# Spacers that move the start addresses of the 256-column matmul operands in retention and attention

## The chip, the cores and the metric

The kernel runs on one core of one Trainium2 chip. The metric is the device time of one execution in microseconds; lower is better. Three timed runs of the kernel before gave a median of 1052.99 us (1051.14 to 1053.38). One more execution was profiled; it took 1049.72 us, of which 1047.6 us lie between its first and its last instruction.

## What is computed

The reference is one encoder layer over 1040 positions (16 learned meta tokens ahead of 1024 inputs) of width 1024, in float32:

```python
u = rms_norm(h);  z = u @ w_in            # one projection of 7680 columns, cut in ten parts
o_r = retention(q, k, v)                  # 4 heads, dk 128, dv 256; chunks of 128; both directions, own decays
y_r = (group_norm(o_r) * silu(rg)) @ w_rb
o_a = attention(q, k, v)                  # 8 heads, 2 key groups, window +-128, 16 meta keys, a sink logit
y_a = (o_a * silu(ag)) @ w_ab
out = (sigmoid(gr) * y_r + sigmoid(ga) * y_a) @ w_o
h + rms_norm(out)                         # meta tokens dropped
```

## The kernel before, in words

Every product of float32 matrices is made of three matmuls, because each operand is split into a high part and a low part: `mm3` (lines 74 to 79) issues high by high (line 76), low stationary by high moving (77) and high stationary by low moving (78) into the same PSUM tile. A matmul first loads its stationary operand, up to 128 columns, into the array (PEld in the profile), and then streams its moving operand, up to 512 columns, through it (PE).

The work stands in three stages. First comes retention (from line 446), one head after the other, with the projections of the next head as filler between its steps. Then comes attention (from line 1360), 32 steps of two heads and 128 queries, with projections of later heads as filler. In the last stage the remaining big projections run as products of 2 by 2 blocks with seven products (`Phase`, from line 935) of 512 columns each. The order of all of it is written out in generators and with `issue_after`; a scheduler puts the instructions into one queue for each engine.

The *core* of retention and attention, as the diff's title has it, is what is neither projection nor transpose. All of its matmuls have a moving operand of 256 columns (1024 bytes in each partition):

- `pa` (stage2 of retention): scores `sh`, `sl` stationary and values `vh`, `vl` moving; then queries `qh`, `ql` stationary and the forward state `Sh`, `Sl` moving.
- `pkv` (the same function): decayed keys `khf`, `klf`, `khb`, `klb` stationary and `vh`, `vl` moving.
- `pb` (the backward loop): `qh`, `ql` stationary and the backward state `Sh`, `Sl` moving.
- `po` (stage3 of attention): values `vah`, `val` and `vm` stationary, and the transposed probabilities `pah`, `pal`, `pbh`, `pbl`, `pm` moving.

The other matmuls are projections (`pk`, `pq`, `pv`, `pak`, `paq`, `pav`, `pe`, and `bz`, `br`, `ba`, `bo` in the last stage; `xh` and `xl` are slices of `big`) and transposes and scores (`tr`, `to`, `pt`, `ps`).

Where a tile lies in a partition is decided by its pool. A pool hands out addresses in the order in which the tags are first asked for; pools of one side stand behind each other. In the kernel before, the tiles of `big` and of the split weights begin at 128 modulo 256 bytes, so 256- and 512-column projections have both of their operands there. The exception is the first piece of the keys, 272 columns wide, whose moving operand begins at 64 modulo 256, with the weights at 128. All moving and all stationary operands of the core begin at 0 modulo 256.

Of the kernel before, what the change touches and what calls it, by code (L numbers as in the profile page):

```python
# [7 lines left out]
F32 = mybir.dt.float32  # L8
# [8 lines left out]
P = 128  # L17
# [17 lines left out]
def cols(c):  # L35
    return (0, NM) if c == 0 else (NM + P * (c - 1), NM + P * c)
# [3 lines left out]
def block_kernel(ctx: ExitStack, tc: tile.TileContext, x0, xT, x, meta, w_in, w_rb, w_ab, w_out, post_w,  # L40
# [33 lines left out]
    def mm3(o, ah, al, bh, bl, first, last, free_group=False):  # L74
        kw = {"skip_group_check": True} if free_group else {}
        nc.tensor.matmul(o, ah, bh, start=first, stop=False, **kw)  # L76
        nc.tensor.matmul(o, al, bh, start=False, stop=False, **kw)  # L77
        latest[:] = [nc.tensor.matmul(o, ah, bl, start=False, stop=last, **kw).ins]  # L78
        return latest[0]
# [8 lines left out]
    def pool_hi(o, i):  # L88
        return nc.gpsimd.tensor_scalar(o, i, 1.0, 1.0, op0=ALU.mult, op1=ALU.mult).ins  # L89

    def dve_lo(o, i, hi):
        return nc.vector.tensor_tensor(o, i, hi.bitcast(F32), ALU.subtract).ins  # L92
# [64 lines left out]
    def projT(w, c, name, mt=None):  # L157
        wh, wl = w
        a, b = cols(c)
        t = pj(name)  # L160
        if c == 0:
            for k in range(KT):
                nc.tensor.matmul(t[0:48, 0:256], xm[:, k, 0:48], wh(k, 0, 256), start=k == 0, stop=False,
                                 skip_group_check=True)
                nc.tensor.matmul(t[0:NM, 0:256], xm[:, k, 0:NM], wl(k, 0, 256), start=False, stop=k == KT - 1,
                                 skip_group_check=True)
            nc.scalar.copy(mt, t[32:32 + NM, 0:256])
            nc.vector.tensor_tensor(mt, t[0:NM, 0:256], mt, ALU.add)
            return mt
        for k in range(KT):  # L170
            mm3(t[0:b - a, 0:256], xh[k][:, a:b], xl[k][:, a:b], wh(k, 0, 256), wl(k, 0, 256), k == 0, k == KT - 1)
        return t

    ra_stack = ExitStack()
    ra = ra_stack.enter_context(tc.tile_pool(name="ra", bufs=1, reuse_waits="tile"))
# [13 lines left out]
    def rope_evac(t, a, b, o, nm):  # L189
# [9 lines left out]
    DT = ra.tile([P, NH, P], F32, name="DT")  # L199
    tabt = ra.tile([P, MW], F32, tag="tb", bufs=1, name="tabt")  # L200
    warm = ra.tile([P, 1], F32, name="warm")
    neg, na, e, e2, s_, ss, acc, lg = (ra.tile([P, 8], F32, name=n) for n in (
        "neg", "na", "e", "e2", "s_", "ss", "acc", "lg"))
    ecst, ex = (ra.tile([P, 28], F32, name=n) for n in ("ecst", "ex"))
    sumsq, ms, r2 = (ra.tile([P, 9], F32, name=n) for n in ("sumsq", "ms", "r2"))
    qd = ra.tile([P, 2 * NH, NB], F32, name="qd")
    kdr = ra.tile([P, 2 * NH, 9], F32, name="kdr")
    nc.vector.memset(warm, 0.0)

    def exponentials(dect):  # L210
# [42 lines left out]
    def evac_qk0(*pieces):  # L253
        if 0 not in qk:
            qk[0] = [], ra.tile([P, 4, 272], F32, tag="kp", bufs=2, name="kr0")
        q, kt = qk[0]
        for i in pieces:
            m0, a, b, t = (outs[2:] + outs[:2])[i]
            if m0:
                o = kt[:, i]  # L260
            else:
                o = ra.tile([P, 512], F32, tag="q", bufs=6, name=f"qr0_{i}")
                q.append(o)
            rot = rope_evac(t, a, b, o, f"qk0_{i}")
        return rot

    with tc.tile_pool(name="setup", bufs=1, reuse_waits="tile") as st:

        head = st.tile([P, 40 + T], F32, name="head")
        dect, idx = head[:, 16:24], head[:, 24:29]  # L270
        xr = [head[:, 40:]] + [st.tile([P, T], F32, tag="xr", bufs=KT - 1, name=f"xr{k}") for k in range(1, KT)]
# [85 lines left out]
        for c in range(9):  # L357
            a, b = cols(c)
            t = st.tile([P, D if c < 7 else T], F32, tag="xn" if c < 7 else "xr", bufs=7 if c < 7 else KT - 1,
                        name=f"xn{c}")[:, 0:D]  # L360
# [7 lines left out]
            rotated = evac_qk0(1)  # L368
        vmeta0 = ra.tile([P, 272], F32, tag="ak", bufs=2, name="vmeta0")[0:NM, 0:256]
        first = [projT(wv0, 0, "pv0_0", vmeta0), projT(wv0, 1, "pv0_1"), projT(wv0, 2, "pv0_2")]  # L370
    with tc.issue_after(rotated):
        turned = evac_qk0(4)
    with tc.issue_after(turned):
# [29 lines left out]
    def kd_(i, c, n):  # L403
        return kdr[0:n, i, c:c + 1]
# [20 lines left out]

    r_stack = ExitStack()
    rp = r_stack.enter_context(tc.tile_pool(name="rp", bufs=1, reuse_waits="tile"))

    def gen_qk(h):
        w = load_w(w_in, U_QK + h)  # L430
        q, kt = [], ra.tile([P, 4, 272], F32, tag="kp", bufs=2, name=f"kr{h}")
        qk[h] = (q, kt)
        for i, (a, b) in enumerate(PIECES):
            t = yield from proj(w, P, a, b, f"pk{h}_{i}")
            rope_late(t, a, b, kt[:, i], f"k{h}_{i}")
            yield
        for i, (a, b) in enumerate(HALVES):
            t = yield from proj(w, 0, a, b, f"pq{h}_{i}")
            o = ra.tile([P, 512], F32, tag="q", bufs=6, name=f"qr{h}_{i}")
            rope_late(t, a, b, o, f"q{h}_{i}")  # L440
            q.append(o)
            yield
# [3 lines left out]
    def retention(h, fill, begin=lambda: None):  # L446
# [11 lines left out]
        def qs(ts, c):  # L458
            return ts[(c - 1) // 4][:, P * ((c - 1) % 4):P * ((c - 1) % 4) + P]

        def ksl(c):
            if c == 0:
                return kt[:, 0, 0:NM]
            i = (c - 1) // 2
            o = P * ((c - 1) % 2) + (NM if i == 0 else 0)
            return kt[:, i, o:o + P]

        def stage1(c):
            n = NM if c == 0 else P
            pv = first.pop(0) if first else projT(wv, c, f"pv{h}_{c}", vmeta)  # L470
            vh = rp.tile([P, 256], R, tag="vh", bufs=4, name=f"vh{h}_{c}")
            vl = rp.tile([P, 256], R, tag="vl", bufs=4, name=f"vl{h}_{c}")
            state["v"] = nc.scalar.copy(vh[0:n], pv[0:n, 0:256]).ins
            state["vl"] = dve_lo(vl[0:n], pv[0:n, 0:256], vh[0:n])
            tr = (p2 if h and c < 2 else p1)(f"tr{h}_{c}")
            nc.tensor.transpose(tr[0:n, 0:P], ksl(c), ident)
            if c > 0:
                nc.tensor.matmul(tr[:, P:2 * P], ksl(c), qs(q, c), start=True, stop=True)
            kd = {}
            for d in ("f", "b"):  # L480
                if d == "f" and c > 7 or d == "b" and c < 2:
                    continue
                sc = kd_(h, c, n) if d == "f" else kd_(NH + h, c, n)
                a = rp.tile([P, P], R, tag="kh" + d, bufs=2, name=f"kh{d}{h}_{c}")
                b = rp.tile([P, P], R, tag="kl" + d, bufs=2, name=f"kl{d}{h}_{c}")
                nc.scalar.activation(a[0:n], tr[0:n, 0:P], AF.Copy, scale=sc)
                nc.vector.scalar_tensor_tensor(b[0:n], tr[0:n, 0:P], sc, a[0:n].bitcast(F32), op0=ALU.mult,
                                               op1=ALU.subtract)
                kd[d] = (a, b)
            s = None  # L490
            if c > 0:
                sd = rp.tile([P, P], F32, tag="sd", bufs=3, name=f"sd{h}_{c}")
                a = rp.tile([P, P], R, tag="sh", bufs=3, name=f"sh{h}_{c}")
                b = rp.tile([P, P], R, tag="sl", bufs=3, name=f"sl{h}_{c}")
                nc.vector.scalar_tensor_tensor(sd, tr[:, P:2 * P], r2[:, c:c + 1], DT[:, h], op0=ALU.mult, op1=ALU.mult)
                nc.scalar.copy(a, sd)
                dve_lo(b, sd, a)
                s = (a, b)
            st1[c] = (n, vh, vl, kd, s)

        def split_state(sr_, nm):
            a = rp.tile([P, 256], R, tag="Sh", bufs=2, name=f"Sh{nm}")
            b = rp.tile([P, 256], R, tag="Sl", bufs=2, name=f"Sl{nm}")
            state["S"] = pool_hi(a, sr_)
            dve_lo(b, sr_, a)
            return a, b

        def stage2(c):
# [21 lines left out]
            if "b" in kd:  # L530
                a, b = kd["b"]
                mm3(pk[:, 256:512], a, b, vh, vl, True, True)
                nc.scalar.copy(kvb[c - 1], pk[:, 256:512])

        stage1(0)
        stage1(1)
        yield
        kvb = [None] + [rp.tile([P, 256], F32, tag="kvb", bufs=NB - 1, name=f"kvb{h}_{c}") for c in range(1, NB)]
# [814 lines left out]
    a_stack = ExitStack()  # L1353
    aw = w_stack.enter_context(tc.tile_pool(name="aw", bufs=1, reuse_waits="tile", side="right"))
    ap = a_stack.enter_context(tc.tile_pool(name="ap", bufs=1, reuse_waits="tile"))
    pm = [ap.tile([P, 256], R, name=f"pm{i}") for i in range(2)]
    for t in pm:
        nc.vector.memset(t.bitcast(F32), 0.0)
# [295 lines left out]
```

## Time and profile before

| what | value |
|---|---|
| three timed runs, median | 1052.99 us (1051.14 to 1053.38) |
| profiled execution | 1049.72 us |
| its span, first to last instruction | 1047.6 us |
| PE busy | 1032.9 us, 99% of the span, 5880 matmuls |
| PEld busy | 906.8 us, 87% |
| DVE, ACT, POOL busy | 838.9, 505.6 and 227.1 us |
| granted TensorE clock | 0.999 of full speed |

The busy time of PE is not the sum of its matmuls' durations. A matmul's record runs from the first column in to the last result out, and the next one begins long before that end. What one matmul costs the kernel is therefore the time from its start to the start of the next, which this document calls its *spacing*; the timeline has the starts. A line of the timeline gives the start in us from the span's start, the duration in us, the engine, the line of the kernel, the operation, and the output and input tiles.

### The profile page before, as it was taken

What the parts mean: (1) busy time and instruction counts of PE and PEld (TensorE: products, weight loads), DVE (VectorE), ACT (ScalarE), POOL (GpSimd) and SP (SyncE); (2) the same over time, 40 slices, a digit from 0 to 9 for tenths busy, and PEclk for the clock granted to TensorE, in tenths of its full rate; (3) what the DMA queues carried; (4) which work ended last, traced back from release to release, by engine and by line L of the source; (5) the groups of instructions that cost most, each with busy time, mean ns of one, the idle gap of its engine ahead of it and who ended that gap; (6) DMA issues with size and microseconds to landing.
All of it is one profiled execution on the core that took longest, in us unless ns stands there. A gap on an engine that the chain in (4) does not pass through costs nothing. (4 is left out here: it accounts for less than half of the span.)

```text
span 1047.6 us, 17241 instructions
## 1 busy us (share of the span) xinstructions
PE 1032.9 (99%) x5880; PEld 906.8 (87%) x5880; DVE 838.9 (80%) x1788; ACT 505.6 (48%) x1127; POOL 227.1 (22%) x338
## 2 busy tenths in 40 slices
PE   8999999999999999999999999999999999999997
PEld 7998999989989888988888888787888788788886
DVE  6876768758876787777778988998899899877665
ACT  5541332522423557665667545455457446334443
POOL 3444244243342423443410000000000000111032
PEclk9999999999999999999999999999999999999999
DMA  9433123233341457665649579999935746789464
GB/s 352 165 85 88 61 45 88 75 71 109 82 99 62 100 153 200 182 168 136 186 153 350 193 255 333 298 328 348 379 131 169 242 171 217 233 224 330 131 121 80
DMA packets 98838, 188.43 MB, mean 180 GB/s; under 512 B 13024, under 2 KB 37632, under 8 KB 98192
## 3 DMA queue, kind: packets, MB, share of 16 engines
q1 hardware_dynamic: 81200, 162.89, 46.5%
q0 software_dynamic: 10176, 14.73, 9.4%
q10 hardware_dynamic: 7376, 9.73, 2.6%
q8 instruction: 46, 0.75, 0.3%
q14 instruction: 40, 0.33, 0.1%
HBM read 124.32 MB, written 57.68 MB: 174 GB/s over the span
## 5 line engine op out<-in xcount | busy, mean ns | idle before, releaser
L1269 POOL DMA_DIRECT2D mx_d<-c1a x4 | 3.6, 888 | 395.2 <-DVE c1a L1260 395.2
L77 PE MATMUL bz<-big,llz 128*128 128x512 f32 x192 | 74.8, 390 | 0.1
L76 PE MATMUL bz<-big,lhz 128*128 128x512 f32 x192 | 74.1, 390 | 0.5 <-ACT lhz L956 0.5
L78 PE MATMUL bz<-big,lhz 128*128 128x512 f32 x192 | 74.2, 389 | 0.0
L76 PE MATMUL pv<-wh,big 128*128 128x256 f32 x256 | 73.6, 288 | 0.0
L77 PE MATMUL pv<-wh,big 128*128 128x256 f32 x256 | 73.5, 287 | 0.0
L78 PE MATMUL pv<-wl,big 128*128 128x256 f32 x256 | 73.5, 287 | 0.0
L77 PE MATMUL bz<-T,llz 128*128 128x512 f32 x176 | 68.6, 390 | 1.1 <-DVE llz L92 1.1
L78 PE MATMUL bz<-T,lhz 128*128 128x512 f32 x176 | 68.5, 389 | 0.0
L76 PE MATMUL bz<-T,lhz 128*128 128x512 f32 x176 | 68.0, 389 | 0.0
L1400 ACT ACTIVATE p<-raw,nm 128x401 f32<-128x401 f32 (+1 forms) x64 | 38.3, 600 | 34.3 <-DVE nm L1397 33.0
L1410 POOL TENSOR_SCALAR p<-p,den 128x400 f32<-128x400 f32 (+1 forms) x60 | 37.7, 684 | 67.8 <-DVE den L1403 65.9
L76 PE MATMUL paq<-big,wh 128*128 128x512 f32 x128 | 51.4, 402 | 0.0
L77 PE MATMUL paq<-big,wl 128*128 128x512 f32 x128 | 50.0, 391 | 0.1
L78 PE MATMUL paq<-big,wh 128*128 128x512 f32 x128 | 50.1, 392 | 0.0
L76 PEld LDWEIGHTS pv<-wh,big 128*128 128x128 f32 x256 | 48.8, 191 | 0.4
L77 PEld LDWEIGHTS pv<-wh,big 128*128 128x128 f32 x256 | 48.8, 191 | 0.4
L78 PEld LDWEIGHTS pv<-wl,big 128*128 128x128 f32 x256 | 48.8, 191 | 0.3
L92 DVE TENSOR_TENSOR wl<-wr,wh 128x1024 fp32r<-128x1024 f32 x28 | 35.0, 1254 | 11.7 <-POOL wh L89 6.6
L76 PEld LDWEIGHTS bz<-big,lhz 128*128 128x128 f32 x192 | 36.0, 188 | 8.6 <-ACT lhz L956 1.3
L77 PEld LDWEIGHTS bz<-big,llz 128*128 128x128 f32 x192 | 36.0, 188 | 7.9 <-DVE llz L92 0.5
L78 PEld LDWEIGHTS bz<-big,lhz 128*128 128x128 f32 x192 | 36.0, 188 | 7.5
(616 smaller groups left out, 3598.5 us busy)
## 6 DMA issues: line engine op xcount, KB each, us to landing
wrz<-in_w_in_dram SPq DMA_DIRECT2D x32, 512.0 KB, 6.0
wr<-in_w_in_dram SPq DMA_DIRECT2D x29, 512.0 KB, 4.1
we<-in_w_in_dram SPq DMA_DIRECT2D x16, 512.0 KB, 4.3
tg<-tg_d SPq DMA_DIRECT2D x32, 256.0 KB, 5.1
e<-e ACTq DMA_DIRECT2D x20, 256.0 KB, 2.6
e<-e SPq DMA_DIRECT2D x20, 256.0 KB, 4.7
xn<-in_x_dram SPq DMA_DIRECT2D x8, 512.0 KB, 9.8
oTr_d<-ost SPq DMA_DIRECT2D x16, 256.0 KB, 2.1
```

The source lines that it names most:

```text
L76: nc.tensor.matmul(o, ah, bh, start=first, stop=False, **kw)
L77: nc.tensor.matmul(o, al, bh, start=False, stop=False, **kw)
L78: latest[:] = [nc.tensor.matmul(o, ah, bl, start=False, stop=last, **kw).ins]
L92: return nc.vector.tensor_tensor(o, i, hi.bitcast(F32), ALU.subtract).ins
L1269: nc.gpsimd.dma_start(d, to, accum_op=ALU.add)
L1400: last["exp"] = nc.scalar.activation(p[:, 0:1 + wid], raw[e_][:, 0:1 + wid], AF.Exp, scale=-1.0, bias=nm_[:, e_:e_ + 1], accum_out=den[:, ...
L1410: nc.gpsimd.tensor_scalar(pt[e_][:, 0:wid], pt[e_][:, 0:wid], den[:, e_:e_ + 1], 1.0, op0=ALU.mult, op1=ALU.mult)
```

## The change

Seven spacer tiles that nobody uses are put into the pools, and nine small tiles of the setup are moved from the long-lived pool `ra` to the pool of the setup. That moves the tiles behind them. No instruction is added or taken away: in the two built programs PE, DVE, ACT and POOL have the same instructions in the same order with the same waits. In SP's queue the order is the same too; the wait for old tiles is moved from one of the first loads of the last stage to the next one at two places (`v` tiles, around the end of attention).

```diff
-    neg, na, e, e2, s_, ss, acc, lg = (ra.tile([P, 8], F32, name=n) for n in (
-        "neg", "na", "e", "e2", "s_", "ss", "acc", "lg"))
-    ecst, ex = (ra.tile([P, 28], F32, name=n) for n in ("ecst", "ex"))
+    lg = ra.tile([P, 8], F32, name="lg")
...
+    ra.tile([P, 56], F32, name="space_ra")
...
+        neg, na, e, e2, s_, ss, acc = (st.tile([P, 8], F32, name=n) for n in (
+            "neg", "na", "e", "e2", "s_", "ss", "acc"))
+        ecst, ex = (st.tile([P, 32], F32, name=n)[:, 0:28] for n in ("ecst", "ex"))
...
+    ra.tile([P, 32], F32, name="space_q")
...
     rp = r_stack.enter_context(tc.tile_pool(name="rp", bufs=1, reuse_waits="tile"))
+    rp.tile([P, 48], F32, name="space_v")
+
+    def space(name, n):
+        if name not in spaces:
+            spaces.append(name)
+            rp.tile([P, n], F32, name=name)
+
+    spaces = []
...
             kd = {}
+            space("space_k", 16)
             for d in ("f", "b"):
...
                 sc = kd_(h, c, n) if d == "f" else kd_(NH + h, c, n)
+                if d == "b":
+                    space("space_b", 16)
...
         def split_state(sr_, nm):
+            space("space_S", 48)
...
     ap = a_stack.enter_context(tc.tile_pool(name="ap", bufs=1, reuse_waits="tile"))
+    ap.tile([P, 48], F32, name="space_p")
```

By the addresses of the two built programs, this is what moves (start modulo 256 bytes):

| operands | before | after |
|---|---|---|
| moving: `vh`, `vl`, `Sh`, `Sl`, `pah`, `pal`, `pbh`, `pbl`, `pm` | 0 | 64 |
| stationary: `sh`, `sl`, `qh`, `ql`, `khf`, `klf`, `khb`, `klb`, `vah`, `val`, `vm` | 0 | 128 |
| `op` (stationary of the transposes `to`), `qr` (moving of the scores in `tr`) | 0 | 128 |
| `p` (stationary of the transposes `pt`), `pm2`, `nm`, `den`, `oa`, `xs` | various | 64 more |
| `kvb`, `S`, `sd` | 0 | 128 |
| `big`, all split weights, `aqh`, `aql`, `kTh`, `kTl`, everything of the last stage | unchanged modulo 256 | unchanged |

## The prediction

> **What bounds the kernel now.** I read the page's engine table first, then PE's waits, then the count of the matmuls whose addresses move, and last the timeline of PE at places where matmuls of different widths and addresses follow each other.
>
> ```profile
> span 1047.6 us, 17241 instructions
> PE 1032.9 (99%) x5880; PEld 906.8 (87%) x5880; DVE 838.9 (80%) x1788; ACT 505.6 (48%) x1127; POOL 227.1 (22%) x338
> PEclk9999999999999999999999999999999999999999
> ```
>
> PE is busy in 99% of the span and the granted clock is full in all slices. The next engine, DVE, has 80%. So PE sets the end, unless it stands idle where the change works. The view of PE's waits says it doesn't:
>
> ```profile
> PE pq L76 <- ACT big L330: 1.6, 2, 1.1
> ...
> PE pt L1427 <- POOL p L1410: 0.5, 2, 0.3
> PE pt L1432 <- DVE pbl L92: 0.3, 1, 0.3
> PE pt L1427 <- DVE pal L92: 0.2, 1, 0.2
> ```
>
> The longest wait is in the setup (1.6 us in total). In the attention stage PE waits 0.5 + 0.3 + 0.2 = 1.0 us, all ahead of transposes. What a matmul of the core gains or loses in spacing is therefore passed on to the end almost whole.
>
> **How many matmuls move.** The view of busy time by tile, over the whole span, gives one row for each output tile of the core, here in the order pa, pb, pkv, po. The number in brackets is the count.
>
> ```profile
> 0.00:1047.00 1047.00, 29.62 (x192) 1.00 0.59 180
> 0.00:1047.00 1047.00, 14.59 (x84) 1.00 0.59 180
> 0.00:1047.00 1047.00, 34.63 (x180) 1.00 0.59 180
> 0.00:1047.00 1047.00, 41.19 (x296) 1.00 0.59 180
> ```
>
> 192 + 84 + 180 + 296 = 752 matmuls. For every one of them the moving operand goes from 0 to 64 modulo 256 bytes and the stationary operand from 0 to 128. One nanosecond of spacing is worth 0.75 us.
>
> **What one costs now.** The durations (283 ns and so on) don't tell it, since the matmuls overlap. The timeline of PE does, by the starts:
>
> ```profile
> 155.82 0.40 PE L77 MATMUL pq<-big,wl 128*128 128x512 f32 x1
> 156.05 0.28 PE L76 MATMUL pa<-vh,sh 128*128 128x256 f32 x1
> ...
> 156.77 0.39 PE L78 MATMUL pq<-big,wh 128*128 128x512 f32 x1
> ...
> 462.08 0.28 PE L78 MATMUL pak<-big,wh 128*128 128x256 f32 x1
> ...
> 462.56 0.28 PE L76 MATMUL po<-pah,vah 128*128 128x256 f32 x1
> ...
> 463.27 0.28 PE L1463 MATMUL po<-pm,vm 128*128 128x256 f32 x1
> 463.39 0.34 PE L76 MATMUL ps<-kTh,aqh 128*128 128x400 f32 x1
> ```
>
> Between 156.05 and 156.77 stand six matmuls of pa, 0.72 / 6 = 120 ns each. Between 462.56 and 463.39 stand seven of po, 0.83 / 7 = 118.6 ns each. I take 119.3 ns, the middle.
>
> There is a second pace at the very same addresses:
>
> ```profile
> 268.60 0.27 PE L78 MATMUL pa<-vl,sh 128*128 128x256 f32 x1
> 268.71 0.28 PE L76 MATMUL pa<-Shf,qh 128*128 128x256 f32 x1
> ...
> 269.30 0.28 PE L77 MATMUL pak<-big,wl 128*128 128x256 f32 x1
> ```
>
> From 268.60 to 269.30 stand six matmuls of 256 columns, four of the core and two of a projection: 0.70 / 6 = 116.7 ns. So 120 ns is not what a matmul of 256 columns must cost. I read it thus: the load for the next matmul runs while this one streams; both read the same memory; how they meet hangs on how their reads lie to each other. At equal addresses modulo 256 the stream mostly settles on 120, and after a break it runs at less for a while.
>
> **What one will cost.** No matmul of 256 columns in this trace has its moving operand at 64. The nearest rows are those of the first key piece: 272 columns, moving at 64, stationary at 128, exactly the new pair of addresses. The run of pak holds twenty of them:
>
> ```profile
> 255.37 0.29 PE L76 MATMUL pak<-big,wh 128*128 128x272 f32 x1
> 255.50 0.29 PE L77 MATMUL pak<-big,wl 128*128 128x272 f32 x1
> 255.63 0.29 PE L78 MATMUL pak<-big,wh 128*128 128x272 f32 x1
> ...
> 257.73 0.29 PE L77 MATMUL pak<-big,wl 128*128 128x272 f32 x1
> ```
>
> From the first to the twentieth start: 2.36 / 19 = 124.2 ns. To bring that to 256 columns I need the cost of a column, from rows of 512:
>
> ```profile
> 152.19 0.39 PE L76 MATMUL pq<-big,wh 128*128 128x512 f32 x1
> ...
> 154.23 0.39 PE L76 MATMUL pq<-big,wh 128*128 128x512 f32 x1
> ```
>
> Nine spacings: 2.04 / 9 = 226.7 ns. The line from 272 to 512 rises by (226.7 - 124.2) / 240 = 0.427 ns per column, so 256 columns lie at 124.2 - 16 x 0.427 = 117.4 ns. That is 1.9 ns under the present 119.3 and close to the faster pace above. I take it.
>
> The bounds of this cost. Below, a matmul can't be spaced closer than its load takes; the transposes, 128 columns, show that:
>
> ```profile
> 459.65 0.60 PE L1427 MATMUL pt<-ident,p 128*128 128x128 f32 x4
> ```
>
> Four of them take 0.60 us from the first start to the last end; a lone one lasts 0.28, so (0.60 - 0.28) / 3 = 107 ns. I don't reach for that, because a stream of 256 columns runs through the same time; half way, 113 ns, is the lowest that I count with. Above, the 272 rows themselves: their first two spacings (255.37, 255.50, 255.63) are 130 ns, 6 over their mean. If that were the new steady state, a matmul would cost 119.3 + 6 = 125.3 ns.
>
> At this step a rule of the Trainium skill speaks against the change. The page "TensorE: Matmul & The Clock Gate", section "Step-by-step: what each phase is for", says that PE has two independent read ports into SBUF, one for the moving and one for the stationary operand. By it their addresses couldn't matter to each other, and the sum would be zero, 1052.99 us. The two paces above, 120 and 116.7 ns at equal width and equal addresses, show that something besides the width decides, but not that it is the addresses; so the trace leaves the rule its chance (below).
>
> **The other parts.** Spacers and moved small tiles issue nothing: no instruction, transfer or wait is added on PE, DVE, ACT or POOL. On SP one load of the last stage waits for old tiles in place of the load before it; those tiles were last used before the end of attention, and the matmuls of the last stage don't read what it loads. I cost it at 0; if that cover were missing, one load's few microseconds would be late once. Operands of DVE, ACT and POOL move too, always by multiples of 32 bytes; these engines are off the path in retention and attention, as PE's waits show, so a change in their durations is hidden up to their slack. DVE has the least: if retention's DVE work were slower, waits on `vl` or `kl` tiles would appear ahead of pkv. The setup's `xr` tiles move as well; the wait of 1.6 us on ACT there is the only place where that could show, so between -0.3 and +0.3 us, taken as 0. In the transposes `to` and `pt` only the stationary operand moves; the four of pt at 459.65 read two tiles of `p` at different offsets already and need 107 ns each, so 0.
>
> Where a 512-column filler hands over to the core there may be a little more. The row at 155.82 lasts 0.40 instead of 0.39 us, and its spacing is 230 ns (155.82 to 156.05) beside 226.7. The next load there is from address 0, later from 128, like all the others. At some 32 such places, an estimate from one per chunk of the rotating heads, 3 ns each are 0.1 us.
>
> **The sum.** 752 x 1.9 = 1.4 us, plus 0.1 us, is 1.5; the faster pace of 116.7 instead of 117.4 would make it 752 x 2.6 = 2.0 plus 0.1. I take the middle, 1.8 us. The profiled execution would go from 1049.72 to 1047.9 us. That execution is 3.3 us under the median of the timed runs, and the same gain goes off both, so the median goes from 1052.99 to 1051.2 us.
>
> **Rivals.**
>
> - *The load and the stream come clear of each other.* Spacing falls to about 113 ns: 752 x 6.3 = 4.7 us, 1048.2 us. For it: the short spells at 116.7 show that 120 holds avoidable time. Against it: the 272 rows, at the new addresses, still stand on the line of the others.
> - *Nothing changes.* Either the addresses don't matter, as by the rule above, or a settled pace of 120 comes back at the new ones: 1052.99 us. For it: projections of 256 columns, with both operands at 128, have the same pace as the core with both at 0: from 462.08 to 462.56 stand four of pak, 0.48 / 4 = 120 ns. That the spacers miss their tiles is no part of this: the built addresses are as stated.
> - *Slower.* With the moving operand 64 bytes behind, its reads meet the load's again and again instead of once, and every matmul of the core costs up to 6 ns more: 752 x 6 = 4.5 us, 1057.5 us. It decides once the new spacing is over 119.3 + 2.8 = 122.1 ns, since 2.8 x 752 is 2.1 us. For it: 272-column matmuls at these very addresses begin their run at 130. Against it: from 255.63 to 257.73 stand seventeen of them at 2.10 / 17 = 123.5 ns, so the high steps are a beginning and no steady state.
>
> **How the numbers follow.** About 0.2%, 2.1 us, is what a measurement of this kernel can tell from no change. The forecast (spacing 116 to 118.5) has a chance of 0.47; its gain of 0.7 to 2.6 us lies on both sides of that bound, and I count 0.29 of it as faster and 0.18 as the same. Coming clear has 0.12, all faster. Nothing changes has 0.19, all the same. Slower has 0.22; small losses hardly fall out of it, so 0.21 slower and 0.01 same. Faster 0.41, same 0.38, slower 0.21. The range has to take in most of the slower rival and of the clear one: 1048.0 to 1056.0 us. The likeliest case's own range is 1050.3 to 1052.3.
>
> **What would show it right or wrong.** In the timeline after, runs of six pa and seven po have 0.70 and 0.82 us from first start to the next tile, not 0.72 and 0.83; PE's busy time falls by about what the span falls; DVE's, ACT's and POOL's busy times stay within a microsecond; projections and the last stage keep 120 and 226.7 ns. If pa and po keep 120 the rule of the ports stands here. If they are faster and the span isn't, waits on DVE tiles ahead of pkv or pt have taken the gain. I am wrong altogether if the span moves and the spacing of the core doesn't.

## The result, and the profile after

The changed kernel takes 1048.43 us (median of 8 runs, 1046.78 to 1049.97), beside 1051.82 us for the kernel before in the same sessions (8 runs, 1050.68 to 1053.38). The ratio is 0.9972 with a 95% interval of 0.9963 to 0.9981: faster by 2.9 us, between 2.0 and 3.9. The forecast was 1.8 us faster, 1051.2 us against a median of 1052.99 us.

The profiled execution of the changed kernel took 1049.97 us, the longest of its eight, and its span isn't shorter than before's. The page:

```profile
span 1047.9 us, 17241 instructions
PE 1032.4 (99%) x5880; PEld 906.3 (86%) x5880; DVE 838.6 (80%) x1788; ACT 505.6 (48%) x1127; POOL 227.0 (22%) x338
```

So the span of this one profile can't carry the verdict; the places where the operands moved can. The timeline of PE in retention, first of the kernel before, then of the kernel after, at the same group of six (the rows that the prediction shows lie one group later):

```profile
149.86 0.28 PE L76 MATMUL pa<-vh,sh 128*128 128x256 f32 x1
...
150.58 0.39 PE L78 MATMUL pq<-big,wh 128*128 128x512 f32 x1
150.81 0.40 PE L76 MATMUL pq<-big,wh 128*128 128x512 f32 x1
151.05 0.39 PE L77 MATMUL pq<-big,wl 128*128 128x512 f32 x1
151.28 0.40 PE L78 MATMUL pq<-big,wh 128*128 128x512 f32 x1
```

```profile
150.29 0.28 PE L76 MATMUL pa<-vh,sh 128*128 128x256 f32 x1
...
151.00 0.39 PE L78 MATMUL pq<-big,wh 128*128 128x512 f32 x1
151.22 0.39 PE L76 MATMUL pq<-big,wh 128*128 128x512 f32 x1
151.45 0.39 PE L77 MATMUL pq<-big,wl 128*128 128x512 f32 x1
```

Six matmuls of pa took 0.72 us and take 0.71 now; to the nanosecond the records say 119, 118, 120, 120, 120, 120 before and 118, 117, 118, 118, 117, 119 after. The second thing to see is what follows. Before, the 512-column projection behind the core needs 230, 236 and 228 ns from start to start (150.58, 150.81, 151.05, 151.28) and its records last 0.40 us at times; after, it runs at 226 and 227 from its first matmul (151.00, 151.22, 151.45).

Over all records, here is the mean spacing of each kind of matmul, from the starts, with spacings that hold a wait left out (over 135 ns at 256 columns, over 245 at 512):

| kind | number | before | after | gain, us |
|---|---|---|---|---|
| core, 256 columns | 752 | 119.23 ns | 117.44 ns | 1.35 |
| 512-column projections of the same stages (pq, paq, pe) | 816 | 228.77 | 228.17 | 0.49 |
| pv, pav, 256 columns | 1040 | 119.21 | 118.83 | 0.40 |
| pk, pak, 256 columns | 432 | 119.29 | 119.01 | 0.12 |

That is 2.4 us, inside the measured 2.0 to 3.9. The core's gain came unevenly: pa went from 119.37 to 117.00 ns, po from 119.56 to 117.37 and pkv from 118.73 to 117.44, while pb stayed at 118.66 and 118.68; its groups of three mostly stand behind value projections at distance 0, and 13 of its 28 groups now begin with two spacings of about 121 ns, which none did before. Of the second row's 0.49 us, some 0.2 are the 38 hand-overs from a filler to the core (two of them from bz, outside this row), which went from 232.3 to 226.9 ns. From the 245th matmul (counted from 0) to the end of the core, the 3769th, 519.2 us became 516.9; two more profiles of kernels with the core's operands at 0 have 518.7 and 518.8 there.

Why then does the span not show it? The profile after starts its 245th matmul at 40.9 us and not at 40.0, and the part behind the core takes 483.1 us and not 481.5. The view of PE's waits has two rows that bear on it:

```profile
PE bz L76 <- DVE u2z L1061: 1.6, 2, 1.3
...
PE pq L76 <- ACT big L332: 1.3, 1, 1.3
```

A wait of 1.6 us for `u2z`, in the last stage, isn't among the waits before. One run below asks whether the change made these.

### The profile page after: what moved, and what is told of

Its sections match the earlier page's. It is cut to its first block, busy times and chain, and to the rows that moved or that the text cites. A ratio compares the mean times of both kernels' runs of the same rounds, so it can differ in the third digit from the quotient of the medians.

```text
span 1047.9 us, 17241 instructions
## 1 busy us (share of the span) xinstructions
PE 1032.4 (99%) x5880; PEld 906.3 (86%) x5880; DVE 838.6 (80%) x1788; ACT 505.6 (48%) x1127; POOL 227.0 (22%) x338
```

## The experiments

All kernels that compute the layer were timed against the kernel before in five rounds. Ratios are to the kernel before; core spacings come from each kernel's own profile, as in the table above.

**Theory.** While a matmul streams its moving operand, the stationary operand of the next one is loaded. The profile of the kernel before has it so: the load for the second matmul of pa begins at 149.87 us, 0.01 us behind the start of the first (149.86 above).

```profile
149.87 0.19 PEld L77 LDWEIGHTS pa<-vh,sl 128*128 128x128 f32 x1
```

The theory is that the two reads disturb each other by the distance of their start addresses (moving minus stationary, modulo 256 bytes). The *distance theory* says that only this distance counts. The *start theory* says that the moving operand's own start counts. The *port theory* says that the addresses don't count at all and the gain came from something else, the moved setup tiles first of all.

### Matmuls alone at 64 pairs of addresses

The kernel `table` keeps nothing of the layer: two copies of some input rows and then only matmuls.

```python
def run(name, n, m, w, count):        # n columns, moving at m, stationary at w modulo 256
    ...
    for a, b in ((wh, mh), (wl, mh), (wh, ml)):
        nc.tensor.matmul(t[:, 0:n], a, b, ...)
...
for i in range(8):
    for j in range(8):
        run("n" + L[i] + L[j], 256, 32 * i, 32 * j, 36)
```

> This kernel leaves the whole computation out: it runs only matmuls over the input's numbers, back to back with no other engine at work, 36 of 256 columns for each of 8 x 8 pairs of start addresses (moving and stationary at 0, 32, ... 224 modulo 256 bytes), 24 of 512 columns for 4 x 4 pairs, 36 of 272 for four, and writes zeros. Distance theory: the spacing hangs on moving minus stationary start modulo 256; all pairs of equal addresses and all pairs 128 apart settle near 120 ns at 256 columns, and all pairs 64 apart, either way, lie near 117. Start theory: it hangs on the moving operand's own start alone, so 64 and 192 give 117 at every stationary start and 0 and 128 give 120. Port theory (the two operands are read independently): all 64 pairs within 1 ns, and the core's gain came from elsewhere.

Three of the groups of instructions of that run; the second letter is the moving start and the third the stationary one, a to h for 0, 32, ... 224:

```profile
L37 PE MATMUL nbb<-mov,sta 128*128 128x256 f32 x36 | 4.5, 283 | 0.0
...
L37 PE MATMUL nbd<-mov,sta 128*128 128x256 f32 x36 | 4.4, 281 | 0.0
...
L37 PE MATMUL nhb<-mov,sta 128*128 128x256 f32 x36 | 4.2, 276 | 0.0
```

The busy time of such a run is 35 spacings and one duration, so `nbb`, equal addresses, has (4.5 - 0.283) / 35 = 120 ns, `nbd`, 64 apart, 118, and `nhb`, moving at 224 and stationary at 32, also 64 apart round the corner, 112 to 113. From the starts, without the first six of each run (four of the eight rows):

| moving \ stationary | 0 | 32 | 64 | 96 | 128 | 160 | 192 | 224 |
|---|---|---|---|---|---|---|---|---|
| 32 | 116.8 | 120.0 | 118.3 | 117.8 | 117.3 | 118.7 | 119.8 | 117.8 |
| 64 | 117.8 | 116.7 | 120.0 | 118.3 | 117.8 | 117.4 | 118.7 | 119.8 |
| 128 | 118.7 | 120.2 | 117.8 | 117.8 | 120.0 | 118.4 | 113.3 | 120.0 |
| 192 | 113.3 | 120.0 | 118.6 | 119.9 | 117.8 | 117.9 | 119.9 | 118.3 |

The rows repeat each other, shifted along, but for a few cells: in the main the number belongs to the distance. Equal addresses settle on 120 in seven of the eight pairs; the first run of the kernel, at 0 and 0, took 213 ns for most of its length and came to 116 to 121 only in its last nine spacings. Distance +96 is no better (119.7 to 120.2). Moving at 64 gives anything from 116.7 to 120, so the start theory falls. At distance -64 (moving 64 below stationary) there are *two* paces, 117.8 in five of the eight pairs and 113.3 in three; -96 has two as well, 117.4 and 120. This kernel can't tell whether the absolute starts pick the pace or how the stream began; the value projections below can. At 512 columns, where four distances were run, equal addresses are the best, 226.6 ns, and -64 is the worst, 233.3 to 233.5: the two widths want different distances.

The rule weighed in the prediction, two independent read ports (the Trainium skill, "TensorE: Matmul & The Clock Gate", section "Step-by-step: what each phase is for"), would make all these pairs alike; with 113.3 to 120.2 ns here the measurement decides against reading it so. Another sentence of the Trainium skill's same page, section "Back-to-back issue gap", says that the spacing of a stream of loads and matmuls is set by both. The trace agrees: with the moving operand at 64, the stationary start alone moves it between 116.7 and 120.0 ns.

### The setup alone, and each half of the change

```diff
-    ra.tile([P, 32], F32, name="space_q")
...
-    rp.tile([P, 48], F32, name="space_v")
...
-            space("space_k", 16)
...
-                    space("space_b", 16)
...
-            space("space_S", 48)
...
-    ap.tile([P, 48], F32, name="space_p")
```

> The changed kernel with the moved setup tiles and the spacer of ra kept, but the other spacers sized so that the core's operands are back at 0 (moving) and 0 (stationary). Both address theories: spacing of the core 119.2 ns, time as before (ratio 0.999 to 1.001). Setup theory (the moved small tiles and x tiles of the setup brought the gain): ratio 0.997.

Measured: ratio 0.9996 (0.9987 to 1.0005), core 119.22 ns. Without the core's spacers nothing is left; the setup theory falls.

The stationary half: `space_q` stays, and the others are sized so that the moving operands lie at 0.

```diff
-    rp.tile([P, 48], F32, name="space_v")
+    rp.tile([P, 32], F32, name="space_v")
...
-            space("space_k", 16)
+            space("space_k", 32)
...
```

> The changed kernel with the stationary half of the change alone: the core's moving operands at 0, its stationary operands at 128. Both address theories: 119 to 120 ns in the core. The hand-over from 512-column fillers (next load from 128 and no longer from 0) keeps its 0.2 us, so a ratio of 0.999 to 1.000. If the stationary start alone decided, 117.2 ns and 0.997.

Measured: 0.9993 (0.9983 to 1.0004), core 119.11 ns, hand-over 226.7 ns. As expected.

The moving half: `space_v`, `space_S` and `space_p` put the moving operands at 64, the stationary ones lie at 0.

```diff
-    ra.tile([P, 32], F32, name="space_q")
...
-    rp.tile([P, 48], F32, name="space_v")
+    rp.tile([P, 16], F32, name="space_v")
...
```

> The changed kernel with the moving half of the change alone: the core's moving operands at 64, its stationary operands at 0, distance +64 and not -64. By groups of six in the 16-byte steps kernel: 118.6 ns and not 117.5, and disturbed fillers behind the core, so about 0.7 us for the core and nothing for the rest; the load for the first core matmul stands 128 off again (232 ns, nothing gained). Ratio 0.9985 to 1.000. Start theory (moving at 64 is what counts): 117.4 ns and 0.997.

Measured: 0.9989 (0.9978 to 0.9999). The core came to 117.47 ns, as good as with the whole change; my 118.6 for it was wrong, and by the core alone the start theory looked as good. But the time doesn't look like the change's, though the intervals just overlap: the hand-overs stay at 232.8 ns, and the 512-column projections among the core stand at 228.97, worse than before's 228.77. So the moving half makes the core faster, but only both halves together make the wide projections faster: 228.78 and 228.97 with one half, 228.17 with both.

Both operands at 64:

```diff
-    ra.tile([P, 32], F32, name="space_q")
+    ra.tile([P, 16], F32, name="space_q")
...
-    rp.tile([P, 48], F32, name="space_v")
...
-            space("space_k", 16)
...
-            space("space_S", 48)
...
```

> The changed kernel with the core's moving operands at 64 and its stationary operands at 64 too. Distance theory: equal addresses, so 119 to 120 ns in the core and a ratio of 0.999 to 1.001. Start theory: moving at 64, so 117.2 ns in the core and a ratio near 0.997.

Measured: 0.9990 (0.9981 to 0.9998), core 118.21 ns. That is between the two theories: 197 of its spacings are 120, the settled pace of equal addresses, where the kernel before, also at equal addresses, has 451. Distance alone thus doesn't give the core's pace. That groups of three to seven end before they settle, so that what the stream comes from counts too, is argued here and not yet shown.

### Steps of 16 bytes, and groups of six behind fillers

```python
for w, c in ((128, "d"), (0, "e")):
    for i in range(16):
        run("u", 512, 128, 128, 6)
        run(c + L2[i], 256, (w + 16 * i) % 256, w, 48)
```

> This kernel leaves the whole computation out, as the table kernel did, and runs matmuls alone: for 16 distances (moving minus stationary start) in steps of 16 bytes, first six matmuls of 512 columns at distance 0, then 48 of 256 columns at the distance, once with the stationary operands at 128 and once at 0; then, for distances 0, 64, 128 and -64, six groups of six matmuls of 256 columns behind six of 512, as the core stands in the kernel. Distance theory: the two halves agree within 1 ns; 0 gives 120; -64 gives 117.8 or, in some runs, the second pace of 113.3 seen once the stream has run in; groups of six give 119 at distance 0 and 117 at -64. Start theory: the two halves differ.

Four of the groups of instructions of this run (d and e: stationary at 128 and at 0; a, h, m: distances 0, +112, -64; 48 matmuls each):

```profile
L37 PE MATMUL da<-mov,sta 128*128 128x256 f32 x48 | 5.9, 283 | 0.0
...
L37 PE MATMUL dm<-mov,sta 128*128 128x256 f32 x48 | 5.8, 281 | 0.0
L37 PE MATMUL eh<-mov,sta 128*128 128x256 f32 x48 | 5.7, 276 | 0.0
...
L37 PE MATMUL em<-mov,sta 128*128 128x256 f32 x48 | 5.6, 276 | 0.0
```

`em` and `dm` have the same distance, -64, and take 5.6 and 5.8 us: `em` ran at 113.3 from its first matmul, `dm` at 117.8 to its last. No spacing in either changed pace in 48 matmuls, so both are stable. The halves differ by more than 1 ns at six of the 16 distances (+128, +80, -112, -96, -64, -48), so the strict distance theory, by which they agree, fails there. Either these distances have several paces each, or the absolute starts count too; this run can't tell.

Groups of six at the distances 0, +64, 128 and -64 gave 118.7, 118.6, 119.5 and 117.5 ns. What stands behind them differs more: the six 512-column matmuls behind a group at distance 0 took 234, 236, 228, 232, 231 and 227 ns each time, behind a group at -64 226 and 227. Behind +64 they took 224 to 241, and behind 128 226 and 227 once and 225 to 240 the other times. This is the ripple of the profiles above: behind a group at distance 0 the wide matmuls need five steps to come back to 227.

### The same distance at other addresses

The core's moving operands at 128, its stationary operands at 192:

```diff
-    ra.tile([P, 32], F32, name="space_q")
+    ra.tile([P, 48], F32, name="space_q")
```

> The changed kernel with the core's moving operands at 128 and its stationary operands at 192: the same distance of -64 at other addresses. Distance theory: 117 to 117.8 ns in the core; but the load for the first core matmul behind a 512-column filler now stands 64 bytes off too, which costs 233 and not 227 ns there (38 times, 0.25 us), so a ratio of 0.997 to 0.999. Start theory: moving at 128 is as before, 119 to 120 ns and a ratio of 0.999 to 1.001.

Measured: 0.9991 (0.9980 to 1.0001), core 117.73 ns. The core is as fast as the distance says, and the start theory fails once more. But the time looks less good than the change's (0.9972), though the intervals overlap. The hand-over was not the reason, against my expectation: it cost 226.2 ns. The fillers are: their first five matmuls behind the core take 233.6, 235.5, 229.0, 232.1 and 231.4 ns, as before the change, where the changed kernel has 228.1, 227.4, 228.3, 226.9 and 227.9. With the core's moving operands at 128, the load of the first filler's weights (at 128) meets the core's last stream at distance 0, and no longer at -64. The absolute addresses count after all. But the distance to the neighbour (from the core's moving start to the filler's weights) isn't all of it: in the two kernels above with moving operands at 64, where that distance is -64 as in the change, the fillers ripple too, with 228.9, 231.3, 231.8, 235.8 and 228.4 ns (stationary at 0) and 233.9, 233.6, 235.5, 225.2 and 231.1 (at 64). Of the six pairs of addresses tried in this kernel, only the change, with -64 in the core and -64 to the filler, has no ripple. Why is not shown.

### The same distance for the value projections

In this kernel the value weights, moving operands of 1040 matmuls of 256 columns, go to 64 too; all others stay.

```diff
+    def w_tile(tag, u, name):
+        t = wp.tile([P, 1088], R, tag=tag, bufs=4, name=name)
+        o = 0 if u in (U_V, U_V + 1, U_V + 2, U_V + 3, U_AV) else 16
+        return t[:, o:o + 1024].rearrange("p (a b) -> p a b", a=4)
...
-        vmeta = rp.tile([NM, 256], F32, tag="vmeta", bufs=2, name=f"vmeta{h}")
+        vmeta = rp.tile([NM, 256], F32, tag="vmeta", bufs=1, name=f"vmeta{h}")
...
```

> The changed kernel with the split weights of the value projections (moving there, 1040 matmuls of 256 columns at distance 0) put at 64 modulo 256, against stationary operands at 128: distance -64 for them too; all other weights stay at 128. Room for it is made by one buffer fewer each for the meta values, the decay tables' scratch, the score tiles and the setup's x tiles. Distance theory: pv and pav fall from 118.8 to 117.4 ns, 1040 x 1.4 = 1.5 us, so a ratio near 0.9958; if their longer runs of 24 reach the second pace of 113.3, up to 5.7 us and 0.992. Rival: the missing buffers add waits that take it back, ratio 0.997 or more.

Measured: 1044.84 us, ratio 0.9939 (0.9927 to 0.9951), faster than both kernels. pv and pav came to 115.65 ns and the core to 116.65. The timeline of PE at one run of 24 matmuls of pav, the tenth and the last, first of the changed kernel, then of this one:

```profile
332.62 0.28 PE L76 MATMUL pav<-wh,big 128*128 128x256 f32 x1
...
334.30 0.28 PE L78 MATMUL pav<-wl,big 128*128 128x256 f32 x1
```

```profile
328.97 0.28 PE L76 MATMUL pav<-wh,big 128*128 128x256 f32 x1
...
330.56 0.28 PE L78 MATMUL pav<-wl,big 128*128 128x256 f32 x1
```

The 14 spacings take 1.68 us there and 1.59 here, 120 and 113.6 ns each. Of the 1040, 483 are now at 113 or 114 and 357 at 117 or 118: both paces of -64 occur at the same two starts (64 and 128, which 980 of the 1040 have), so the absolute starts don't pick between them. What goes with the pace is the stream ahead. Of the unbroken runs of ten or more, 19 follow a core matmul (at -64 too) without a gap, and all keep its pace: behind a last core spacing of 113 or 114 nine of nine end at 113.2 to 113.5, behind 117 to 119 ten of ten end at 117.5 to 118.0. Of the 26 runs whose first spacing is 200 ns or more, 18 come to the fast pace and 8 stay at 117 to 118. The core gains from it as well: 215 of its spacings are at 113 or 114, where the change has 125, and pb, which stands between value projections, falls from 118.68 to 116.23 ns.

The page has it in the span:

```profile
span 1041.7 us, 17241 instructions
PE 1027.6 (99%) x5880; PEld 902.7 (87%) x5880; DVE 838.1 (80%) x1788; ACT 505.9 (49%) x1127; POOL 227.6 (22%) x338
```

The same buffers taken away, with the value weights at 128 (`o = 16` for all):

> The same kernel as v64 with the same buffers taken away, but with the value weights at 128 like all others. It prices the buffers alone: without cost, the ratio is that of the change, 0.997; pv and pav stay at 118.8 ns.

Measured: 0.9975 (0.9966 to 0.9985), pv and pav 118.92 ns, core 117.41. The buffers cost nothing that can be measured; the addresses bring all of it.

Two more distances for the value weights, `v240` and then `v16`:

```diff
-        o = 0 if u in (U_V, U_V + 1, U_V + 2, U_V + 3, U_AV) else 16
+        o = 44 if u in (U_V, U_V + 1, U_V + 2, U_V + 3, U_AV) else 16
...
+        o = 52 if u in (U_V, U_V + 1, U_V + 2, U_V + 3, U_AV) else 16
```

> As v64, but the value projections' moving weights at 240 modulo 256: distance +112 to their stationary operands at 128. In the 16-byte steps both chains at +112 ended at 113.3 ns, but only after ten to twenty matmuls at 117 to 120. If the kernel's runs of 24 get there as late, pv and pav lie at 115 to 117 ns and the ratio at 0.993 to 0.996, no better than v64 (115.65 ns, 0.9939). If the second pace, once reached, is carried over from run to run, 113.5 ns and 0.992.

> As v64, but the value weights at 16 modulo 256: distance -112. In the 16-byte steps one chain ran at 113.3 from its first matmul and the other at 118.7 throughout, so by what the stream comes from: between 113.5 and 118.7 ns, ratio 0.992 to 0.997. A distance that is no multiple of 64 has to be as good or as bad as the steps say, or what was measured alone doesn't carry over to the kernel.

Measured: 0.9968 (0.9957 to 0.9979) for both, with 116.89 and 118.14 ns. Both are inside what the 16-byte steps allowed, except that the ratio at +112 is just worse than expected, and neither beats -64.

### The kernel before once more

> The kernel before, unedited, profiled and timed once more. In the profile before, the 245th matmul starts at 40.0 us; in eight of the nine profiles of changed kernels that keep the moved setup tiles it starts at 40.5 to 41.4, and most wait 0.5 to 1.6 us for a u2 tile in the last stage, where before waits for none. If the moved setup tiles cost that, this run starts its 245th matmul at 40.0 again and has no such wait. If it is scatter from execution to execution, it lies at 40.5 to 41.4 or waits there too. Core spacing 119.2 ns in either case; ratio 0.999 to 1.001.

Measured: ratio 0.9995 (0.9986 to 1.0004), core 119.22 ns. Its 245th matmul starts at 40.7 us. Its waits:

```profile
PE pq L76 <- ACT big L330: 1.2, 1, 1.2
...
PE bz L76 <- DVE u2z L1046: 0.7, 1, 0.7
```

The unedited kernel has the late start and the wait for `u2z` as well. They scatter from execution to execution; the 40.0 us of the first profile was early, and nine of the ten profiles of edited kernels lie at 40.5 to 41.4. The part behind the core scatters too, from 481.3 to 483.3 us over the twelve profiles, and its shortest is that of a kernel with all of the change's moved tiles (stationary at 192).

### All runs against the starts

Summing the four kinds of the first table for each kernel, from its own profile, and setting it beside the measured time:

| kernel | core, ns | sum of the four kinds, us | measured, us (ratio x 1051) |
|---|---|---|---|
| before_again | 119.22 | 0.1 | -0.5 (-1.5 to 0.4) |
| m0w0 | 119.22 | 0.0 | -0.4 (-1.4 to 0.5) |
| m0w128 | 119.11 | -0.5 | -0.7 (-1.8 to 0.4) |
| m64w64 | 118.21 | -0.9 | -1.1 (-2.0 to -0.2) |
| m128w192 | 117.73 | -1.4 | -0.9 (-2.1 to 0.1) |
| m64w0 | 117.47 | -1.6 | -1.2 (-2.3 to -0.1) |
| v128 | 117.41 | -2.3 | -2.6 (-3.6 to -1.6) |
| the change | 117.44 | -2.4 | -2.9 (-3.9 to -2.0) |
| v16 | 117.09 | -3.4 | -3.4 (-4.5 to -2.2) |
| v240 | 117.12 | -4.6 | -3.4 (-4.5 to -2.2) |
| v64 | 116.65 | -6.3 | -6.4 (-7.7 to -5.1) |

All sums but one lie in the measured interval, and that of v240 lies 0.1 us outside. Within the intervals, about 1 us to either side, the spacing of matmuls accounts for the times; no other gain or loss is needed. The core's spacing itself repeats closely: 119.23, 119.22 and 119.22 in three profiles with its operands at 0 and 0, 117.44 and 117.41 in two at 64 and 128.

## Why the prediction was right, point by point

- *What bounds the kernel*: right. PE is busy in 99% of the span after as well, and what the spacing gained was passed on: sums by the starts and measured times agree in the table above.
- *752 matmuls move, at 119.3 ns each*: right; the mean of all was 119.23. That each gains 1.9 ns was right of the mean alone: the 84 of pb gained nothing.
- *The new cost, 117.4 ns, read off the 272-column rows at the same two addresses*: right to 0.1 ns, 117.44. It was luck in part. The matmuls alone show that -64 has two paces, 113.3 and 117.8, and the core mixes them with run-in spacings of up to 125 ns. And the line from which it was read joins two distances: the 272 rows are at -64, the 512 rows at 0. By `table`, at -64 alone, 272 columns take 123.3 ns and 512 take 233.4, and that line would have given 116.0.
- *The reading of the two paces*: right that the relation of load and stream decides. That equal addresses settle on 120 was confirmed at seven of the eight equal pairs of `table` and at both of `steps16`.
- *Slower, because the reads meet again and again*: the 130 ns at the head of the 272 rows were a run-in and no steady state, as the prediction held against it; by `table`, 64 and 128 are the best of the four pairs tried at 272 columns (123.3 ns, the others 125.2 to 126.7). Nothing at 256 columns settled above 120.2.
- *Nothing changes, by the rule of the ports*: refuted, for these operands, by `table`. Nor did a settled 120 come back at the new addresses: 11 of the core's spacings are 120 ns after, 451 were before.
- *Coming clear to 113 ns*: didn't happen to the change, where 125 of the 752 spacings are 113 or 114. The pace exists, though, and the value projections reach it in half of their matmuls in `v64`.
- *The sum*: too small, 1.8 us for a measured 2.9 (2.0 to 3.9). The core's term held (1.4 us forecast from the rows, 1.35 found). The term that was mis-sized is that of the neighbours. I gave the hand-over 0.1 us (32 places, 3 ns each) and it brought 0.2 (38 places, 5.4 ns each); and I gave the projections behind the core nothing, where the wide ones brought 0.3 us more and the narrow ones 0.5. The rows that show the ripple (0.40 in place of 0.39 us behind a core group) were in view, and I used them for the hand-over alone. The median after, 1048.43 us, is nearer to the clear rival's 1048.2 than to the forecast 1051.2; in part that is because the three runs of the kernel before on which the forecast rests had a median 1.2 us above that of all eight. It is the rows and not the time that decide for the forecast's mechanism.
- *What would show it*: pa fell from 0.72 to 0.71 us per six, near the 0.70 named, and the 25 unbroken groups of six went from 717 to 702 ns on the mean; po, with 0.82 us for seven, is as named. PE's busy time fell by 0.5 us where the span rose by 0.3, so that sign failed in this one profile. "Projections keep 120 and 226.7 ns" failed: they gained 0.3 to 0.6 ns each.
- *The setup at 0*: right; 0.9996 for it alone.

What stays open: which of the two paces a run falls into behind a gap (18 of 26 took the faster in `v64`), since no run here forced it. Nor is shown why the ripple stays away at one pair of starts alone, or what in the memory repeats every 256 bytes.

## What to carry to other kernels

Where PE is the bound and its matmuls of 256 columns are spaced near 120 ns, look at the start addresses of moving and stationary operands modulo 256 before looking at the schedule. Here equal starts settled on 120 ns at 256 columns, among the worst tried, and on 226.6 at 512, the best of four distances; moving 64 bytes below stationary gave 117.8 or 113.3 at 256. Count all matmuls of that width before choosing which to move; here the value projections were more than the core and brought more. And choose the absolute addresses with the neighbours in view: a group's last stream runs beside the next group's first load, and at -64 a run without a gap ahead kept the pace of what it followed.

## What the runs showed of the hardware

Spacing at 256 columns depends in the main on the distance of the operands' starts modulo 256 bytes, in a range from 113.3 to 120.2 ns, with the pattern shifted along when both move, but for a few cells (`table`). At least one distance holds two stable paces, 113.3 and 117.8 at -64, for 48 matmuls on end (`steps16`). A run without a gap ahead kept the pace of the stream before it, at the same distance of -64, in 19 of 19 cases (`v64`). At 512 columns the range is 226.6 at equal addresses to 233.5 at -64 (`table`). Behind a group of six at equal addresses the next five wide matmuls take 228 to 236 ns and not 227 (`steps16`).
